# Rotary queries and the scaling of attention weights moved to GpSimd, with a group's rotary queries made first

## The chip, the cores and the metric

The kernel runs on one core of a Trainium2 chip. The metric is the device time of one execution in microseconds; lower is better. The core has five engines that run at the same time, each through its own queue in strict order: TensorE (PE in the profile; its weight loads are PEld), VectorE (DVE), ScalarE (ACT), GpSimd (POOL) and SyncE (SP), which issues the DMAs. An instruction that has to wait for another engine holds up everything behind it on its own queue.

## What is computed

The reference is a trunk of two layers on 256 tokens of width 2048, in fp32: a Conformer convolution module and an MLP, then multi-head latent attention and an MLP, with RMS norms in between. The change lies in the attention layer:

```python
def mla(h, cos, sin, w_in, q_norm_g, kv_norm_g, w_q_up, w_kv_up, w_o):
    down = h @ w_in
    c_q, c_kv, k_pe = jnp.split(down, [Q_LORA_RANK, Q_LORA_RANK + KV_LORA_RANK], axis=-1)
    q = (rms_norm(c_q, q_norm_g) @ w_q_up).reshape(B, S, N_HEADS, QK_NOPE_DIM + QK_ROPE_DIM)
    q_nope, q_pe = jnp.split(q, [QK_NOPE_DIM], axis=-1)
    q_pe = apply_rope(q_pe, cos[:, :, None, :], sin[:, :, None, :])
    k_pe = apply_rope(k_pe, cos, sin)
    kv = (rms_norm(c_kv, kv_norm_g) @ w_kv_up).reshape(B, S, N_HEADS, QK_NOPE_DIM + V_HEAD_DIM)
    k_nope, v = jnp.split(kv, [QK_NOPE_DIM], axis=-1)
...
    s = (jnp.einsum('bqhd,bkhd->bhqk', qn, k_nope)
         + jnp.einsum('bqhr,bkr->bhqk', qp, k_pe)).astype(jnp.float32) * scale
...
    p = jax.nn.softmax(s, axis=-1).astype(v.dtype)
    return jnp.einsum('bqhk,bkhd->bqhd', p, v)
```

There are 16 heads; a head's query has 128 plain columns (`q_nope`) and 64 rotary ones (`q_pe`). The rotary turn of a query's halves x1 and x2 is x1·cos − x2·sin and x2·cos + x1·sin: four multiplications, a subtraction and an addition.

## The kernel before, in words

**Numbers in two parts.** Matrix products are made in fp32r from a high and a low part of each operand, in three products (`mm3`, L178: high·high, low·high, high·low). The high part is a copy on ScalarE (`hi_part`, L186; for weights L154), the low part a subtraction on DVE (`lo_part`, L191; for weights L155). Each weight block is therefore loaded by DMA, then split in two halves (`split_half`, L148), each a ScalarE instruction followed by a DVE instruction. In the convolution, some of the low parts are made on GpSimd (also L155); in the attention layer GpSimd has nothing to do.

**Units and pieces.** The attention weights are listed as `units` in the order in which they are used (L848 to L878). `start_unit` notes that the halves of the unit two places further on are due; `prefetch` (L909) issues those splits, and the load of a unit three further on behind a second half. The 16 heads are treated in four groups of four. For each group there are 14 pieces of TensorE work, each 12 matrix products of 256 columns into one PSUM tile (`acc`, six banks in rotation):

- `qn_piece` (L1000), four: the plain query of one head, and its two parts (L186, L191);
- `qp_piece` (L1015), two: the rotary queries of the group's four heads for one half of the tokens. `rope` (L828) turns them by six DVE instructions of 128 columns (L834 to L839), the four multiplications reading the products from PSUM. `hi_part` and `lo_part` make the two parts, in the tile `qhl`;
- `kv_piece` (L973), eight: keys (L987 to L990, two parts) or values (L995 to L998).

`qp_turn` (L1029) transposes the rotary queries of two heads on TensorE (L1034), and ScalarE copies them into `qpA` and `qpB` (L1043, L1044).

**Heads.** `scores` (L1060) makes a head's 3 × 128 columns of scores, DVE takes the maxima (`mx`, L1075 and L1076) and ScalarE the exponentials with their sums (`pr`, L1078). `weights` (L1083) inverts the sums and scales the exponentials (two DVE instructions, of 128 and 256 columns, L1088). `weights_turn` (L1090) transposes them (L1094) and copies them to `pT` (L1096); `values` (L1098) multiplies them with the values (L1103, L1104) and makes the two parts `oh` and `ol`.

**The order** is written out by hand (`manual_schedule`, L1124 to L1242), and every engine's queue follows it. The pieces of group g + 1 are spread over the heads of group g. One head h issues: scores(h), one piece, the turn of weights(h − 1), for the last two heads of a group `qp_turn`, values(h − 2), the scaling of weights(h), and the rest of its pieces, each followed by a `prefetch` of one half. Before the first head stand group 0's pieces and the first three pieces of group 1. In `q_work` (L1049) the four `qn` pieces come first and the two `qp` pieces second. The pieces of the last group's heads (12 to 15) are those of the output projection.

Of the kernel before, what the change touches and what calls it, by code (L numbers as in the profile page):

```python
# [10 lines left out]
F32 = mybir.dt.float32  # L11
# [7 lines left out]
P = 128  # L19
# [53 lines left out]
def trunk_kernel(  # L73
# [750 lines left out]
    with ExitStack() as cx:  # L824
        at = cx.enter_context(tc.tile_pool(name="at", bufs=1, reuse_waits="tile"))
        at2 = cx.enter_context(tc.tile_pool(name="at2", bufs=2, reuse_waits="tile"))

        def rope(dst, src, t, nh):  # L828

            a, b = src[:, :, 0:HR], src[:, :, HR:DR]  # L830
            cb = cos[:, t : t + 1, :].broadcast_to([P, nh, HR])
            sb = sin[:, t : t + 1, :].broadcast_to([P, nh, HR])
            m = [at2.tile([P, 4, HR], F32, tag=f"m{i}", name=nm("m"), bufs=1)[:, :nh, :] for i in range(4)]
            nc.vector.tensor_tensor(m[0], a, cb, op=ALU.mult)  # L834
            nc.vector.tensor_tensor(m[1], b, sb, op=ALU.mult)
            nc.vector.tensor_tensor(m[2], b, cb, op=ALU.mult)
            nc.vector.tensor_tensor(m[3], a, sb, op=ALU.mult)
            nc.vector.tensor_tensor(dst[:, :, 0:HR], m[0], m[1], op=ALU.subtract)
            nc.vector.tensor_tensor(dst[:, :, HR:DR], m[2], m[3], op=ALU.add)  # L839

        HG = 4
        NG = H // HG
# [7 lines left out]
        def unit(key, srcs, shape):  # L850
            pieces[key] = len(units)
            units.append((srcs, shape))
# [9 lines left out]

        def q_units(g):
            hs = slice(g * HG, (g + 1) * HG)
            unit(("qn", g), [wq4[:, j : j + 1, hs, :DN] for j in range(NJ)], [P, NJ, HG * DN])
            unit(("qp", g), [wq4[:, j : j + 1, hs, DN:] for j in range(NJ)], [P, NJ, HG * DR])

        for g in range(NG):
            if g == 0:
# [145 lines left out]
        def qp_piece(g, t):  # L1015
            key = ("qp", g)
            start_unit(key, t)
            o = acc_tile()[:, : HG * DR]
            ts = slice(t * P, (t + 1) * P)
            for j in range(NJ):  # L1020
                wh, wl = w_at(key, j)
                mm3(o, qh[:, j, ts], ql[:, j, ts], wh, wl, j == 0, j == NJ - 1)
            qp = at2.tile([P, HG, DR], F32, tag="qp", name=nm("qp"))
            rope(qp, o.rearrange("p (h n) -> p h n", h=HG), t, HG)
            hl = qps[g, t] = at2.tile([P, HG, 2, DR], F32R, tag="qhl", name=nm("qhl"))
            hi_part(qp, hl[:, :, 0, :])
            lo_part(qp, hl[:, :, 0, :], hl[:, :, 1, :])

        def qp_turn(g, m):  # L1029

# [16 lines left out]
            return [lambda i=i, c=c: kv_piece(g, i, c) for i in range(HG // 2) for c in range(4)]  # L1047

        def q_work(g):  # L1049
            return [lambda i=i: qn_piece(g, i) for i in range(HG)] + [lambda t=t: qp_piece(g, t) for t in range(T)]  # L1050

        def group_work(g):
            kv = kv_work(g)
# [29 lines left out]
        def weights(h):  # L1083
            pr, zs = prs[h], zss.pop(h)
            nc.vector.reciprocal(zs, zs)
            for t, at_, n in sides:
                q = pr[:, at_ : at_ + n]
                nc.vector.tensor_scalar(q, q, scalar1=zs[:, t : t + 1], scalar2=None, op0=ALU.mult)  # L1088

        def weights_turn(h):  # L1090
            pr = prs.pop(h)
# [32 lines left out]
        with tc.manual_schedule():  # L1124
            for n in range(3):
                u_load(n)
            for n in range(LOOK):
                u_split(n, 0)
                u_split(n, 1)
                u_load(n + 3)  # L1130

            ckv = at.tile([P, T, KR + DR], F32, tag="cx", name="ckv")
            ps = [[acc_tile() for _ in range(2)] for _ in range(T)]
            for k in range(KC):
                u, j = divmod(k, 2)
                start_unit(("kv", u), j)
                prefetch()
                if k == KC - 4:
                    r = rms_rstd(ssq, NNB, D, "n")
                wh, wl = w_at(("kv", u), j)  # L1140
                for t in range(T):
                    for i in range(2):
                        ns = slice(i * NKV, (i + 1) * NKV)
                        mm3(ps[t][i][:, :NKV], xh_kt(k, t), xl_kt(k, t), wh[:, ns], wl[:, ns], k == 0, k == KC - 1)
            for t in range(T):
                for i in range(2):
                    nc.scalar.activation(
                        ckv[:, t, i * NKV : (i + 1) * NKV], ps[t][i][:, :NKV], AF.Copy, scale=r[:, t : t + 1]
                    )
            ps = [acc_tile() for _ in range(T)]  # L1150
            for k in range(KC):
                u, j = divmod(k, 4)
                if j in (0, 2):
                    start_unit(("q", u), j // 2)
                    prefetch()
                wh, wl = w_at(("q", u), j)
                for t in range(T):
                    mm3(ps[t], xh_kt(k, t), xl_kt(k, t), wh, wl, k == 0, k == KC - 1)
                if k == 0:
                    sq = squares(ckv, KR)  # L1160
                if k == 3:
                    normed(ckv, KR, sq)
                    kps = []
                    for t in range(T):
                        kp = at2.tile([P, 1, DR], F32, tag="kp", name=nm("kp"))
                        rope(kp, ckv[:, t : t + 1, KR:], t, 1)
                        hhl = at2.tile([P, 3, DR], F32R, tag="hhl", name=nm("hhl"))
                        for i in range(2):
                            hi_part(kp[:, 0, :], hhl[:, i, :])
                        lo_part(kp[:, 0, :], hhl[:, 0, :], hhl[:, 2, :])  # L1170
                        kps.append(hhl.rearrange("p a b -> p (a b)").bitcast(F32))
                if k == 9:
                    to_T(ckv, 0, kvh_k, kvl_k, g_kv)
                if k == 11:
                    to_T(ckv, 2, kvh_k, kvl_k, g_kv)
                if k == 13:
                    pt = tr_tile()
                    for t in range(T):
                        nc.tensor.transpose(pt[:, t * P : (t + 1) * P], kps[t][:, : 2 * DR], ident)
                        nc.tensor.transpose(pt[:DR, S + t * P : S + (t + 1) * P], kps[t][:, 2 * DR :], ident)  # L1180
                    nc.scalar.activation(kpA, pt[:, :S], AF.Copy)
                    nc.scalar.activation(kpB[:DR, :], pt[:DR, S:], AF.Copy)
            cq = at.tile([P, T, QR], F32, tag="cx", name="cq")
            for t in range(T):
                nc.scalar.activation(cq[:, t, :], ps[t], AF.Copy, scale=r[:, t : t + 1])
            sq = squares(cq, QR)
            gp.append(right_pool("gp", 2))
            work = kv_work(0)
            for w in work[:2]:
                w()  # L1190
                prefetch()
            normed(cq, QR, sq)
            for w in work[2:6]:
                w()
                prefetch()
            to_T(cq, 0, qh_k, ql_k, g_q)
            to_T(cq, 2, qh_k, ql_k, g_q)
            for w in work[6:] + q_work(0):
                w()
                prefetch()  # L1200
            work = group_work(1)
            warm(AF.Exp)
            work[0]()
            for m in range(2):
                qp_turn(0, m)
            for w in work[1:3]:
                prefetch(1)
                w()
            work = work[3:]
            for g in range(NG):  # L1210
                for i in range(HG):
                    h = g * HG + i

                    n = -(-len(work) // (HG - i))
                    todo, work = work[:n], work[n:]
                    scores(h)
                    todo.pop(0)()


                    if h > 0:  # L1220
                        weights_turn(h - 1)
                    if i > 1 and g + 1 < NG:
                        qp_turn(g + 1, i - 2)
                    if h > 1:
                        values(h - 2)
                    weights(h)
                    prefetch(1)
                    for w in todo:
                        w()
                        prefetch(1)  # L1230
                if g + 2 < NG:
                    work = group_work(g + 2)
                elif g + 2 == NG:
                    work = [lambda k=k: o_piece(k) for k in range(H - HG)]
            weights_turn(H - 1)
            values(H - 2)
            for k in (H - 4, H - 3):
                o_piece(k)
            values(H - 1)
            for k in (H - 2, H - 1):  # L1240
                o_piece(k)
            prefetch()  # L1242
# [53 lines left out]
```

## Time and profile before

| | us |
|---|---|
| time, median of 3 runs (lowest, highest) | 2030.07 (2029.39, 2031.12) |
| the profiled execution, its own time | 2029.38 |
| its span, first to last instruction | 2027.6 |
| granted TensorE clock over the span | 0.998 |
| PE busy | 1995.5 |
| DVE busy | 1225.6 |
| ACT busy | 962.6 |
| POOL busy | 173.9 |

The attention layer's groups lie between about 1093 and 1262 us of the span. In a row of the timeline the first number is the start, the second the duration, then engine, line, operation, output<-inputs, partitions and shapes, the count, and in brackets the idle time before it with what ended it. A row of the stretches gives its length, then for each engine busy time and instructions, the granted clock, the DMA's busy share and its rate. A row of the waits gives who waited for whom, the sum, the number of waits and the longest.

### The profile page before, as it was taken

Reading aid. Unit: us, or ns where it says so; the run is one execution under the profiler, and the core shown is the slowest. Engines: PE = TensorE matmul, PEld = TensorE weight load, DVE = VectorE, ACT = ScalarE, POOL = GpSimd, SP = SyncE. Lnnn points to the kernel's source line nnn. Section 1 sums busy time; section 2 is a strip of 40 time slices with the busy share of each in tenths; the row PEclk is TensorE's granted clock in tenths of the full one; section 3 lists DMA queues with packets and bytes.
Section 4 is the critical chain, followed back from the end, with each engine's and each line's share of the span. In section 5 each row is a group of like instructions: output and inputs, shape, how many; then the busy total and the mean of one; then the engine's idle time right before and its main releaser. Section 6 shows DMA issues by size and latency. Waiting matters only on the chain.

```text
span 2027.6 us, 27995 instructions
## 1 busy us (share of the span) xinstructions
PE 1995.5 (98%) x11150; PEld 1747.5 (86%) x11150; DVE 1225.6 (60%) x1858; ACT 962.6 (47%) x1364; POOL 173.9 (9%) x101
## 2 busy tenths in 40 slices
PE   7999999999999999999999899999999999999998
PEld 7999888888888888888889898888888888888886
DVE  5999866665544466555546675665554445565454
ACT  5444665544433354444445554554443334454442
POOL 5887400000000000000000000000000000000000
PEclk9999999999999999999999999999999999999999
DMA  7555355665555666655555335566655566555553
GB/s 235 167 167 166 122 190 171 203 188 187 191 199 191 188 189 192 194 192 187 187 162 175 111 125 180 179 204 189 193 197 188 191 200 191 187 187 190 200 191 104
DMA packets 243267, 367.59 MB, mean 181 GB/s; under 512 B 15416, under 2 KB 89792, under 8 KB 242880
## 3 DMA queue, kind: packets, MB, share of 16 engines
q1 hardware_dynamic: 242400, 364.68, 56.9%
q8 instruction: 87, 1.43, 0.3%
q10 hardware_dynamic: 736, 1.12, 0.2%
q14 instruction: 44, 0.36, 0.1%
HBM read 363.68 MB, written 2.10 MB: 180 GB/s over the span
## 4 chain that ended last, share of the span: by engine, by line
PE 92%; DVE 4%; ACT 2%; issue 1%; DMA 0%; SPq 0%; DVEq 0%; ACTq 0%
PE acc L397 23%; PE acc L180 15%; PE acc L182 15%; PE acc L181 15%; PE acc L398 12%; PE acc L484 3%; PE acc L482 3%; PE acc L483 3%; DVE lo L155 1%; PE sum L515 1%; PE tr L237 1%; ACT hi L154 0%; ACT pr L1078 0%; DMA xs<-in_x 0%; DVE mx L1075 0%
## 5 line engine op out<-in xcount | busy, mean ns | idle before, releaser
L155 DVE TENSOR_TENSOR lo<-raw,hi 128x1024 fp32r<-128x1024 f32 (+1 forms) x628 | 755.3, 1206 | 679.8 <-ACT hi L154 667.3
L154 ACT ACTIVATE hi<-raw 128x1024 fp32r<-128x1024 f32 (+1 forms) x696 | 722.8, 1046 | 788.9 <-PE acc L181 455.3
L397 PE MATMUL acc<-xt,hi 128*128 128x512 f32 x2048 | 710.6, 390 | 0.0
L398 PE MATMUL acc<-xt,lo 128*128 128x256 f32 x2048 | 577.7, 282 | 0.0
L397 PEld LDWEIGHTS acc<-xt,hi 128*128 128x128 f32 x2048 | 384.5, 188 | 80.5
L180 PE MATMUL acc<-hi,gh 128*128 128x512 f32 x1024 | 398.6, 389 | 0.0
L182 PE MATMUL acc<-lo,gh 128*128 128x512 f32 x1024 | 398.4, 389 | 0.0
L181 PE MATMUL acc<-hi,gl 128*128 128x512 f32 x1024 | 398.4, 389 | 0.0
L398 PEld LDWEIGHTS acc<-xt,lo 128*128 128x128 f32 x2048 | 387.1, 189 | 0.1
L182 PEld LDWEIGHTS acc<-lo,gh 128*128 128x128 f32 x1024 | 192.2, 188 | 40.0
L180 PEld LDWEIGHTS acc<-hi,gh 128*128 128x128 f32 x1024 | 192.2, 188 | 39.7
L181 PEld LDWEIGHTS acc<-hi,gl 128*128 128x128 f32 x1024 | 192.2, 188 | 39.7
L549 DVE SCALAR_TENSOR_TENSOR sum<-ub,w_dw,sum 128x256 f32<-128x256 f32 x402 | 167.6, 483 | 4.9 <-ACT sum L518 2.9
L155 POOL TENSOR_TENSOR lo<-raw,hi 128x1024 fp32r<-128x1024 f32 x68 | 161.9, 2403 | 57.8 <-ACT hi L154 57.8
L482 PE MATMUL acc<-xt,hi 128*128 128x256 f32 x512 | 147.3, 288 | 0.0
L484 PE MATMUL acc<-xt,lo 128*128 128x256 f32 x512 | 143.2, 280 | 0.2 <-POOL lo L155 0.2
L483 PE MATMUL acc<-xt,hi 128*128 128x256 f32 x512 | 143.0, 279 | 0.0
L483 PEld LDWEIGHTS acc<-xt,hi 128*128 128x128 f32 x512 | 96.3, 188 | 0.6 <-DVE xt L193 0.2
L482 PEld LDWEIGHTS acc<-xt,hi 128*128 128x128 f32 x512 | 96.3, 188 | 0.4
L484 PEld LDWEIGHTS acc<-xt,lo 128*128 128x128 f32 x512 | 96.2, 188 | 0.4 <-POOL lo L155 0.4
L918 POOL MEMSET pad_kv<- 128x8 f32 x1 | 0.1, 104 | 772.5 <-PE acc L182 772.5
L405 ACT ACTIVATE v<-acc 128x256 f32<-128x256 f32 x128 | 46.4, 382 | 25.3 <-PE acc L398 25.3
(215 smaller groups left out, 1767.8 us busy)
## 6 DMA issues: line engine op xcount, KB each, us to landing
raw<-in_mlp_w SPq DMA_DIRECT2D x256, 1024.0 KB, 5.2
raw<-in_conv_w_pw SPq DMA_DIRECT2D x64, 512.0 KB, 5.0
raw<-in_conv_w_pw SPq DMA_DIRECT2D x16, 1024.0 KB, 5.0
raw<-in_mla_w_o SPq DMA_DIRECT2D x16, 1024.0 KB, 5.6
raw<-in_mla_w_kv_up SPq DMA_DIRECT2D x8, 1024.0 KB, 5.4
raw<-in_mla_w_in SPq DMA_DIRECT2D x8, 576.0 KB, 3.7
raw<-in_mla_w_in SPq DMA_DIRECT2D x4, 1024.0 KB, 5.6
raw<-in_mla_w_q_up SPq DMA_DIRECT2D x16, 256.0 KB, 3.2
```

The costliest lines, as they stand in the source:

```text
L154: nc.scalar.activation(hi, raw[:, js, :], AF.Copy)
L155: eng.tensor_tensor(lo, raw[:, js, :], hi.bitcast(F32), op=ALU.subtract)
L180: nc.tensor.matmul(ps, sh, mh, start=start, stop=False)
L181: nc.tensor.matmul(ps, sl, mh, start=False, stop=False)
L182: nc.tensor.matmul(ps, sh, ml, start=False, stop=stop)
L397: nc.tensor.matmul(ps[b], wh[:, bs], xhl(k), start=k == 0, stop=False)
L398: nc.tensor.matmul(ps[b][:, :S], wl[:, bs], xh(k), start=False, stop=k == KC - 1)
L405: nc.scalar.activation(v[:, b, :], o[:, S:], AF.Copy)
L482: nc.tensor.matmul(o, wh[:, bs], xh(k), start=k == 0, stop=False)
L483: nc.tensor.matmul(o, wh[:, bs], xl(k), start=False, stop=False)
L484: nc.tensor.matmul(o, wl[:, bs], xh(k), start=False, stop=k == KC - 1)
L549: nc.vector.scalar_tensor_tensor(out=out, in0=ubs[c][:, w : w + S], scalar=tap(c, w), in1=pcs[c], op0=ALU.mult, op1=ALU.add)
```

## The change

Three things are changed.

1. The rotary turn of the queries goes to GpSimd. GpSimd's instructions are given SBUF operands only, so a new ScalarE copy first brings the products from PSUM into a tile `qr` of one buffer. The low part of the rotary queries goes to GpSimd as well; the high part stays on ScalarE. `qp` has one buffer instead of two. The keys' rotary turn stays on DVE.
2. The two scaling instructions of each head's weights go to GpSimd; the reciprocal stays on DVE.
3. In a group, the two `qp` pieces come ahead of the four `qn` pieces, and the two units of weights change places in the list. Before the first head, group 0's `qp_turn` comes ahead of group 1's first piece.

```diff
-        def rope(dst, src, t, nh):
+        def rope(dst, src, t, nh, eng):
...
-            nc.vector.tensor_tensor(m[0], a, cb, op=ALU.mult)
-            nc.vector.tensor_tensor(m[1], b, sb, op=ALU.mult)
-            nc.vector.tensor_tensor(m[2], b, cb, op=ALU.mult)
-            nc.vector.tensor_tensor(m[3], a, sb, op=ALU.mult)
-            nc.vector.tensor_tensor(dst[:, :, 0:HR], m[0], m[1], op=ALU.subtract)
-            nc.vector.tensor_tensor(dst[:, :, HR:DR], m[2], m[3], op=ALU.add)
+            eng.tensor_tensor(m[0], a, cb, op=ALU.mult)
+            eng.tensor_tensor(m[1], b, sb, op=ALU.mult)
+            eng.tensor_tensor(m[2], b, cb, op=ALU.mult)
+            eng.tensor_tensor(m[3], a, sb, op=ALU.mult)
+            eng.tensor_tensor(dst[:, :, 0:HR], m[0], m[1], op=ALU.subtract)
+            eng.tensor_tensor(dst[:, :, HR:DR], m[2], m[3], op=ALU.add)
...
         def q_units(g):
             hs = slice(g * HG, (g + 1) * HG)
+            unit(("qp", g), [wq4[:, j : j + 1, hs, DN:] for j in range(NJ)], [P, NJ, HG * DR])
             unit(("qn", g), [wq4[:, j : j + 1, hs, :DN] for j in range(NJ)], [P, NJ, HG * DN])
-            unit(("qp", g), [wq4[:, j : j + 1, hs, DN:] for j in range(NJ)], [P, NJ, HG * DR])
...
-            qp = at2.tile([P, HG, DR], F32, tag="qp", name=nm("qp"))
-            rope(qp, o.rearrange("p (h n) -> p h n", h=HG), t, HG)
+
+            qr = at2.tile([P, HG, DR], F32, tag="qr", name=nm("qr"), bufs=1)
+            nc.scalar.activation(qr, o.rearrange("p (h n) -> p h n", h=HG), AF.Copy)
+            qp = at2.tile([P, HG, DR], F32, tag="qp", name=nm("qp"), bufs=1)
+            rope(qp, qr, t, HG, nc.gpsimd)
             hl = qps[g, t] = at2.tile([P, HG, 2, DR], F32R, tag="qhl", name=nm("qhl"))
             hi_part(qp, hl[:, :, 0, :])
-            lo_part(qp, hl[:, :, 0, :], hl[:, :, 1, :])
+            nc.gpsimd.tensor_tensor(hl[:, :, 1, :], qp, hl[:, :, 0, :].bitcast(F32), op=ALU.subtract)
...
         def q_work(g):
-            return [lambda i=i: qn_piece(g, i) for i in range(HG)] + [lambda t=t: qp_piece(g, t) for t in range(T)]
+            return [lambda t=t: qp_piece(g, t) for t in range(T)] + [lambda i=i: qn_piece(g, i) for i in range(HG)]
...
             for t, at_, n in sides:
                 q = pr[:, at_ : at_ + n]
-                nc.vector.tensor_scalar(q, q, scalar1=zs[:, t : t + 1], scalar2=None, op0=ALU.mult)
+                nc.gpsimd.tensor_scalar(q, q, scalar1=zs[:, t : t + 1], scalar2=None, op0=ALU.mult)
...
             work = group_work(1)
             warm(AF.Exp)
-            work[0]()
             for m in range(2):
                 qp_turn(0, m)
+            work[0]()
```

## What was predicted, before the run

> **What bounds the kernel now.** I read the page's engine line, then busy time by stretch, then PE's waits inside the attention layer.
>
> ```profile
> span 2027.6 us, 27995 instructions
> PE 1995.5 (98%) x11150; PEld 1747.5 (86%) x11150; DVE 1225.6 (60%) x1858; ACT 962.6 (47%) x1364; POOL 173.9 (9%) x101
> ...
> 1118.20:1139.50 21.30, 17.38 (x148) 17.18 (x148) 12.98 (x36) 11.97 (x27) 0.00 (x0) 1.00 0.35 90
> 1139.50:1145.70 6.20, 6.10 (x36) 5.79 (x37) 4.36 (x10) 3.54 (x10) 0.00 (x0) 0.72 0.59 182
> 1145.70:1262.00 116.30, 113.33 (x782) 104.52 (x782) 76.09 (x185) 64.12 (x148) 0.00 (x0) 1.00 0.45 145
> ...
> PE tr L1094 <- DVE pr L1088: 6.6, 3, 4.0
> PE tr L1034 <- DVE qhl L191: 2.3, 1, 2.3
> ```
>
> TensorE is busy 98% of the span, so the end moves only by what TensorE waits. In the attention layer it waits 2.3 us for group 0's rotary queries, and 6.6 us in three waits for scaled weights. After the longest (4.0 us) its granted clock averages 0.72 for 6.2 us, about 1.7 us more. All a gain can take is thus about 10.6 us. GpSimd is empty here and DVE and ScalarE are about 65% and 55% busy: neither is full, but each runs in strict order, and what is late is the head of a queue.
>
> **What the edits cost as work.** DVE and ScalarE rows of before; first number the start, second the duration:
>
> ```profile
> 1121.73 1.06 ACT L154 ACTIVATE hi<-raw 128x1024 fp32r<-128x1024 f32 x1
> 1122.68 0.38 ACT L186 ACTIVATE qTh<-acc 128x256 fp32r<-128x256 f32 x1
> ...
> 1126.62 0.37 ACT L1078 ACTIVATE pr<-acc,mx 128x128 f32<-128x128 f32 x1 [2.35 <-DVE mx L1076]
> ...
> 1127.42 0.38 ACT L186 ACTIVATE qTh<-acc 128x256 fp32r<-128x256 f32 x1
> 1130.20 0.42 ACT L186 ACTIVATE qhl<-qp 128x256 fp32r<-128x256 f32 x1 [2.40 <-DVE qp L839]
> 1130.53 1.04 ACT L154 ACTIVATE hi<-raw 128x1024 fp32r<-128x1024 f32 x1
> 1122.83 1.23 DVE L155 TENSOR_TENSOR lo<-raw,hi 128x1024 fp32r<-128x1024 f32 x1 [2.44 <-ACT hi L154]
> 1123.97 0.42 DVE L191 TENSOR_TENSOR qTl<-acc,qTh 128x256 fp32r<-128x256 f32 x1
> 1124.30 1.22 DVE L155 TENSOR_TENSOR lo<-raw,hi 128x1024 fp32r<-128x1024 f32 x1
> ...
> 1125.77 0.61 DVE L1075 TENSOR_REDUCE mx<-acc 128x1 f32<-128x128 f32 x2
> ...
> 1128.18 0.16 DVE L1085 RECIPROCAL zs<-zs 128x2 f32<-128x2 f32 x1
> 1128.37 0.55 DVE L1088 TENSOR_SCALAR pr<-pr,zs 128x128 f32<-128x128 f32 x2
> 1128.84 0.28 DVE L834 TENSOR_TENSOR m<-acc,cos 128x128 f32<-128x128 f32 x1
> ...
> 1129.83 0.28 DVE L839 TENSOR_TENSOR qp<-m,m 128x128 f32<-128x128 f32 x1
> ```
>
> Instructions follow each other closer than they last, so I use slots, start to start: ScalarE half split 0.95, eviction 0.28, qhl hi 0.33, the two exponentials 0.80; DVE half split 1.14, L191 0.33, from the maximum's start to the exponential 0.85, scaling pair 0.47. A rotary turn on DVE takes 1.27 (1128.84 to 1130.11). A hand-over is 0.04 (1122.79 to 1122.83).
>
> DVE loses eight times 1.27 and a lo part of about 0.42, and sixteen scaling pairs: 13.5 + 7.5 = 21 us. ScalarE gains eight copies out of PSUM (0.38 as L186, slot 0.28). None of this is itself on the path: neither engine is full. The price of GpSimd comes from the convolution:
>
> ```profile
> 107.77 1.30 POOL L689 TENSOR_TENSOR xs<-xs,b 128x512 f32<-128x512 f32 x1
> 109.00 0.14 POOL L496 MEMSET ub<- 128x30 f32 x1
> ...
> 113.44 7.14 POOL L155 TENSOR_TENSOR lo<-raw,hi 128x1024 fp32r<-128x1024 f32 x3 [0.34 <-ACT hi L154]
> ...
> 0.80 0.20 POOL masks.py:197 MEMSET ident<- 128x128 f32 x1
> ...
> 16.94 2.58 POOL L155 TENSOR_TENSOR lo<-raw,hi 128x1024 fp32r<-128x1024 f32 x1 [0.63 <-ACT hi L154]
> ...
> 16.80 3.01 DVE L627 TENSOR_SCALAR xn<-xs,y 128x512 f32<-128x512 f32 x2
> ...
> 21.30 0.86 DVE L627 TENSOR_SCALAR xn<-xs,y 128x512 f32<-128x512 f32 x2
> ```
>
> A two-input slot is 1.23 for 512 columns and about 2.37 for 1024 (7.14 less 2.40, halved), a straight line with 0.09 + 0.00223 a column: 0.375 for 128, 0.66 for 256. A rotary turn is then 6 × 0.375 = 2.25, with tail and two hand-overs **R = 2.45 us**, against DVE's 1.27. No 128-column two-input row exists: below, six memset-like 0.20 give R 1.4; above, six at the 256-column price give 4.1. I take the line. A scaling pair lies between 0.4 (two memsets) and 1.04 (two-input slots); I take 0.65, and only head 0 has it on the path.
>
> Side by side the engines disturb each other: two L627 took 3.01 us while GpSimd's 16.94 ran, alone 0.86, so one was held for the whole GpSimd instruction. Does DVE's half split (two SBUF inputs) likewise hold a rotary multiply that starts after it? No row shows it. Not held: 0. Held: up to 0.9 us at each second turn of a group, because a 1.14 us half split starts just before the copy ends. I take held, as L627 is the nearest row, and keep both ends. The Trainium skill, SBUF — State Buffer, "Who interferes with whom", speaks against this change too: a DVE instruction with two SBUF inputs and a GpSimd instruction that reads SBUF exclude each other, and the later blocks. By it the sum is the held one; without it, the other.
>
> **What moves.** ScalarE's hi part of the rotary queries (L186) stands right behind the new copy, so ScalarE sits still for R twice in every group, and behind it queue the half splits, the evictions that free PSUM banks, and the next exponentials. The same wait for DVE's turn stands in before's list:
>
> ```profile
> ACT qhl L186 <- DVE qp L839: 14.7, 8, 2.5
> ```
>
> That is 1.8 each, with no copy ahead of it; by R it becomes eight times 2.45, about 20. The waits also come earlier: the rotary pieces are first in the group, so for group 1 both stand ahead of head 0's exponentials, where before they stood behind. The weight loads on SP are as many, two units changing places; no wait of this layer names a DMA, and loads run three units ahead: nothing.
>
> PE rows, and three of ScalarE's:
>
> ```profile
> 1105.77 0.28 PE L1010 MATMUL acc<-qh,hi 128*128 128x256 f32 x1
> ...
> 1118.16 1.28 ACT L214 ACT_TABLE_LOAD   x1
> ...
> 1119.83 0.59 ACT L1043 ACTIVATE qpA<-tr 128x512 fp32r<-128x512 f32 x1
> ...
> 1118.13 0.98 PE L1034 MATMUL tr<-ident,qhl 128*128 128x128 f32 x7 [2.25 <-DVE qhl L191]
> ...
> 1121.75 0.22 PE L180 MATMUL acc<-kTh,qTh 128*128 128x128 f32 x1
> ...
> 1122.90 0.28 PE L1010 MATMUL acc<-qh,hi 128*128 128x256 f32 x1
> ...
> 1124.31 0.28 PE L180 MATMUL acc<-hi,qh 128*128 128x256 f32 x1
> ...
> 1139.60 0.70 PE L1094 MATMUL tr<-ident,pr 128*128 128x128 f32 x3 [4.02 <-DVE pr L1088]
> ...
> 1151.06 0.23 PE L180 MATMUL acc<-kTh,qTh 128*128 128x128 f32 x1
> ...
> 1155.00 0.37 ACT L1078 ACTIVATE pr<-acc,mx 128x128 f32<-128x128 f32 x1 [2.28 <-DVE mx L1076]
> ...
> 1177.60 0.61 PE L1094 MATMUL tr<-ident,pr 128*128 128x128 f32 x3 [1.28 <-DVE pr L1088]
> ```
>
> A piece of work is 1.40 us of PE (1122.90 to 1124.31), scores 1.15 (1121.75 to 1122.90), a transpose 0.11 (seven in 0.98, the last one's 0.27 taken off): 0.35 and 0.44 for three and four; values, four matmuls at a twelfth of a piece or less, about 0.4.
>
> Group 0 starts at 1105.77. Its two rotary pieces now end at 1107.2 and 1108.6. From 1107.37: copy 0.38, R, hi 0.33, half split of 512 columns (about 0.5, half of 0.95), copy 0.38, a hold of 0.4 by that short split, R, hi 0.42, lo 0.66 and hand-overs: the turn can start at 1115.5, while PE has its four other pieces done at 1114.2. The wait is 1.3 instead of 2.25, and scores(0) starts at 1120.65 instead of 1121.75: **-1.1**.
>
> Groups 0 to 1. ScalarE reaches the table load about when it did, at 1118.16; 1.4 later follow the four qpA/qpB copies (1.90 from 1119.83 to 1121.73 before), without the eviction at 1119.56: done at 1121.45. Copy to 1121.83, R: hi at 1124.28, half split to 1125.67, copy to 1125.94; the turn is held until 1126.85: hi at 1129.25, half split to 1130.64, DVE's half to 1131.82, L191, maximum at 1132.16, exponential at 1133.0 (before: 1126.62). PE has scores(1) done at 1127.15; the next kv piece lacks that half split and the bank of qn(1,0), waits until 1132.2 (5.0 us) and ends at 1133.6; weights(0) scaled at 1135.45, 1.85 more. Behind exponential(0) stand two evictions and two half splits of each engine: maximum(1) at 1138.15, exponential(1) at 1139.0, eviction, the turned weights, reciprocal at 1140.7, the pair on GpSimd by 1141.4. So weights(1) turn at 1141.45 instead of 1139.5. The wait of 4.0 and its low clock are replaced: the low clock now falls mostly into time when PE waits anyway (I leave 0.6 of 1.7 visible, an estimate). From there to scores(4) PE has two weight turns, two query turns, two values, four pieces and a scores, 9.2: 1151.2 against 1151.06, **+0.15** in all; the 1.1 is spent.
>
> Groups 1 to 2, from scores(4) as 0. Exponential at 3.85 as now (1155.00 less 1151.06); 0.80, copy, R: hi 7.48 to 7.81; evictions of turned weights and values, 384 and 256 columns, 0.65 by L186's 0.28; half split 8.46 to 9.52; copy to 9.79; held until 10.7: hi 13.1; half split to 14.49; eviction, half split; DVE frees the first qn bank at 16.0. PE stands at the kv piece that reuses it at 13.05 (two scores 2.3, six pieces 8.4, two weight turns and values 1.55, and 0.8 for weights(3)): 3.0 us of wait. Eviction, half split and maximum follow on DVE: exponential(5) at 19.5, which frees the bank of scores(6) at 20.35; PE, done with two kv pieces at 18.95, waits another 1.4. From there scores, piece, weight turn, query turn, values, two pieces, scores, piece are 9.1: weights(6) turn at 29.45. Before it was 26.54 (1177.60 less 1151.06), 1.28 of wait included: **+2.9**.
>
> Groups 2 to 3 repeat it (before's 1.28 stands there too): **+2.9**. The later heads have no rotary work and microseconds of slack: 0. After the layer everything shifts whole. Sum 0.15 + 2.9 + 2.9 = **+6.0 us**.
>
> The profiled execution took 2029.38 (span 2027.6 and 1.8 around it); the median is 2030.07, 0.7 above. 2029.4 + 6.0 + 0.7 = **2036.1 us**.
>
> **Rivals.** *Not held*: each second turn is 0.9 shorter, group 1 reaches scores(4) 1.2 earlier, groups 2 and 3 cost 2.1 each: about +3, 2033, within 0.2%. For it: L155 isn't L627.
>
> *Dearer turn*: R near 3.6 (a 0.57 slot, the 32-column pieces of the operands costing extra, or every multiply held). Twice 1.15 in three groups, +7 on the sum: 2043. A low clock after each new 3 us wait (it came after 4.0, not after 2.25) would add up to 2 a group. The Trainium skill, TensorE: Matmul & The Clock Gate, Part 1, puts that point at about 3.4 us of idling, just above my 3.0; the 2.25 and the 4.0 agree with it, and no row lies between.
>
> *Faster*: GpSimd's short instructions cost like DVE's, R about 1.4, nothing held. Then group 0's 2.25 disappears, both 1.28 too, and of the 4.0 and its 1.7 two waits of about 1.8 are left (the chain to the kv piece and to weights(0), two turns shorter): 2.25 + 2.56 + 2.1 = 6.9 less, 2023. It decides from R about 1.85, a slot of 0.28. Against it: both longer GpSimd rows lie on a line that gives 0.375. *The change doesn't act*, i.e. DVE's 21 us and the waits cancel: 2030; nothing singles it out.
>
> **How the numbers follow.** A measurement can tell about 0.2% (4 us) from no change. Chances: forecast, with its spread, 0.47; dearer 0.22; not held 0.16; no effect 0.06; faster 0.09. Of the forecast's 0.47, 0.05 falls below 2034.1, and not held and no effect are within 0.2%. So faster 0.09, same 0.27, slower 0.64. The range runs from near no change to dearer with some low clock: 2029 to 2046.
>
> **What would show it.** Right: GpSimd TENSOR_TENSOR of 128 columns near 0.4 us; ScalarE's qhl hi parts waiting on GpSimd's qp, about 2.4 us each; PE waiting at a kv piece in head 1 (about 5 us) and again in heads 5 and 9, not at L1094 for DVE; a GpSimd multiply beside L155 lasting 1 us or more. Wrong: multiplies of 0.25 us, or ScalarE's eight waits no longer than the 14.7 us of before.

## The result, and the profile after

The changed kernel takes **2042.45 us** (median of 4 runs, 2041.34 to 2043.62) against 2030.12 for the kernel before on the same chip: a ratio of 1.0063 (95% interval 1.0051 to 1.0076), **12.3 us slower**. The forecast was 2036.1, slower, with 2029 to 2046 as its range: the sign and the range hold, but the loss is twice the forecast's 6.0. The profiled execution took 2041.34.

The page's engine line. DVE is 19 us less busy, as the cost of the edits in work had it (21), and PE's idle time has grown:

```profile
span 2039.5 us, 28020 instructions
PE 1999.1 (98%) x11150; PEld 1750.2 (86%) x11150; DVE 1206.5 (59%) x1770; ACT 964.6 (47%) x1372; POOL 239.4 (12%) x189
```

PE's waits in the attention layer: three at the first key piece (L987) of heads 1, 5 and 9, seven for scaled weights, now from GpSimd, and the one of group 0's turn. Their sum is 17.2 us, against 8.9 in the two rows of before that stand in the prediction.

```profile
PE acc L987 <- DVE qTl L191: 10.8, 3, 4.9
PE tr L1097 <- POOL pr L1091: 5.0, 7, 1.6
PE tr L1037 <- POOL qhl L1030: 1.4, 1, 1.4
```

The stretches of heads 5 and 9: besides the waits, the granted clock (the column behind POOL) is low here too, not only behind the wait in head 1 (0.86 from 1126 to 1150). 0.91 over 20 us is 1.8 us of work not done.

```profile
1160.00:1180.00 20.00, 16.70 (x125) 16.16 (x124) 10.73 (x23) 11.52 (x30) 8.20 (x12) 0.91 0.41 120
...
1200.00:1220.00 20.00, 16.31 (x120) 15.56 (x119) 12.35 (x25) 12.07 (x28) 5.71 (x10) 0.91 0.48 158
```

PE's L987 names DVE, but what DVE's queue waited for stands in the list of all engines: 40.2 us for ScalarE's half splits, against 17.5 in the same stretch of before; and ScalarE 25.7 us for GpSimd's turn (14.7 for DVE's before). Before's row first, then after's two:

```profile
DVE lo L155 <- ACT hi L154: 17.5, 16, 2.4
```

```profile
ACT qhl L186 <- POOL qp L839: 25.7, 8, 4.3
...
DVE lo L155 <- ACT hi L154: 40.2, 25, 6.1
```

ScalarE's rows in head 0 show the chain itself. Each copy for GpSimd is made (the second, at 1125.97, is left out here), and ScalarE then sits 2.66 and 3.39 us in front of the high part; the half split (L154) that the key piece of head 1 needs stands behind it:

```profile
1121.66 0.37 ACT L1025 ACTIVATE qr<-acc 128x256 f32<-128x256 f32 x1
1124.69 0.42 ACT L186 ACTIVATE qhl<-qp 128x256 fp32r<-128x256 f32 x1 [2.66 <-POOL qp L839]
...
1129.72 0.42 ACT L186 ACTIVATE qhl<-qp 128x256 fp32r<-128x256 f32 x1 [3.39 <-POOL qp L839]
1130.05 1.04 ACT L154 ACTIVATE hi<-raw 128x1024 fp32r<-128x1024 f32 x1
```

On GpSimd, the groups by form: an instruction of a turn mostly takes 0.46 us; the two instructions of a scaling 0.60 and 1.80 on average (128 and 256 columns), the second of them often lengthened by DVE's work, as a later section shows.

```profile
L1091 POOL TENSOR_SCALAR pr<-pr,zs 128x256 f32<-128x256 f32 x16 | 28.8, 1799 | 0.0
...
L1091 POOL TENSOR_SCALAR pr<-pr,zs 128x128 f32<-128x128 f32 x16 | 9.7, 603 | 78.8 <-DVE zs L1088 57.8 <-PE acc L1076 15.3 <-PE acc L182 5.7
...
L838 POOL TENSOR_TENSOR qp<-m,m 128x128 f32<-128x128 f32 x8 | 3.7, 457 | 0.0
```

### The profile page after: what moved, and what is told of

Its sections match the earlier page's. It is cut to its first block, busy times and chain, and to the rows that moved or that the text cites. A ratio compares the mean times of both kernels' runs of the same rounds, so it can differ in the third digit from the quotient of the medians.

```text
span 2039.5 us, 28020 instructions
## 1 busy us (share of the span) xinstructions
PE 1999.1 (98%) x11150; PEld 1750.2 (86%) x11150; DVE 1206.5 (59%) x1770; ACT 964.6 (47%) x1372; POOL 239.4 (12%) x189
## 4 chain that ended last, share of the span: by engine, by line
PE 93%; DVE 2%; ACT 2%; POOL 1%; issue 1%; DMA 0%; SPq 0%; DVEq 0%; ACTq 0%; POOLq 0%
PE acc L397 23%; PE acc L182 15%; PE acc L181 15%; PE acc L180 15%; PE acc L398 12%; PE acc L484 3%; PE acc L482 3%; PE acc L483 3%; PE sum L515 1%; PE tr L237 1%; ACT hi L154 1%; DVE lo L155 1%; POOL pr L1091 0%; DMA xs<-in_x 0%; PE acc L987 0%
## 5 line engine op out<-in xcount | busy, mean ns | idle before, releaser
L155 DVE TENSOR_TENSOR lo<-raw,hi 128x1024 fp32r<-128x1024 f32 (+1 forms) x628 | 756.8, 1208 | 706.9 <-ACT hi L154 694.9
L154 ACT ACTIVATE hi<-raw 128x1024 fp32r<-128x1024 f32 (+2 forms) x696 | 722.6, 1045 | 789.1 <-PE acc L181 455.3
```

The source lines that it names most:

```text
L154: nc.scalar.activation(hi, raw[:, js, :], AF.Copy)
L155: eng.tensor_tensor(lo, raw[:, js, :], hi.bitcast(F32), op=ALU.subtract)
```

## The experiments

Three theories are told apart. **A**: ScalarE's high part of the rotary queries waits for GpSimd's long turn at the head of ScalarE's queue, and what stands behind it is late; the scaling adds a little. **B**: GpSimd's work itself costs, above all the scaling, which stands between the exponentials and the turn of the weights, and the contention with DVE. **C**: the new order of a group does it. All differences are against the kernel before on the same chip (2029.41 in the first four, 2029.36 in the next four, 2029.67 in the last two).

**Only the scaling on GpSimd** (part 2 of the change):

```diff
-                nc.vector.tensor_scalar(q, q, scalar1=zs[:, t : t + 1], scalar2=None, op0=ALU.mult)
+                nc.gpsimd.tensor_scalar(q, q, scalar1=zs[:, t : t + 1], scalar2=None, op0=ALU.mult)
```

> Only the scaling of the weights goes to GpSimd; rotary turn and order as before. Theory A (ScalarE stands behind GpSimd's rotary turn, and that is most of the 12 us): a small loss, about +3 us, since the three waits for scaled weights of before grow by 1 to 1.5 us each (the pair takes at least 1.5 us in the changed kernel's trace, 0.55 on DVE). Rival B (the scaling on GpSimd, 1.5 to 3.3 us a pair, is the main cost): +8 us or more. Rival C (the new order is the main cost): about 0.

Measured 2034.70, a ratio of 1.0026 (1.0016 to 1.0036): +5.3. PE's waits:

```profile
PE tr L1094 <- POOL pr L1088: 9.4, 8, 2.3
PE tr L1034 <- DVE qhl L191: 2.3, 1, 2.3
```

Three waits for weights (6.6 us) have become eight. The result lies between A's +3 and B's +8: the scaling is dearer than A had it, but it doesn't carry the whole loss, as B would have it.

**Only the rotary turn on GpSimd** (part 1; order and scaling as before): the scaling, `q_units`, `q_work` and the group-0 turn are put back. Against the changed kernel:

```diff
-            return [lambda t=t: qp_piece(g, t) for t in range(T)] + [lambda i=i: qn_piece(g, i) for i in range(HG)]
+            return [lambda i=i: qn_piece(g, i) for i in range(HG)] + [lambda t=t: qp_piece(g, t) for t in range(T)]
...
-                nc.gpsimd.tensor_scalar(q, q, scalar1=zs[:, t : t + 1], scalar2=None, op0=ALU.mult)
+                nc.vector.tensor_scalar(q, q, scalar1=zs[:, t : t + 1], scalar2=None, op0=ALU.mult)
...
+            work[0]()
             for m in range(2):
                 qp_turn(0, m)
-            work[0]()
```

> Only the rotary turn of the queries (with its copy and its low part) goes to GpSimd; scaling on DVE, plain queries first as before. Theory A: +5 us: group 0's turn, now right behind its GpSimd work, waits about 2 us longer than 2.25, and the three waits for weights grow by about 1 us each. Rival B: +1 us or less. Rival C (GpSimd's turn does harm only in the new order): within 1 us of before.

Measured 2042.48, 1.0066 (1.0053 to 1.0079): +13.1, far more than any theory said. PE's waits:

```profile
PE tr L1037 <- POOL qhl L1030: 10.6, 4, 3.8
PE tr L1097 <- DVE pr L1091: 7.0, 3, 4.0
```

In the old order the rotary queries are made last and needed soon, so PE waits for the turned queries themselves: twice at group 0's turn and once each for those of groups 2 and 3, 10.6 us in all. The granted clock is 0.83 from 1120 to 1160, where before has 1.00 and 0.91 in the two halves. The waits for weights, which A had growing, stay as they were (7.0 against 6.6). So this is another wait than the one that A names: it shows that the turn on GpSimd is dear without the scaling, against B's +1, but it doesn't decide between A and C for the changed kernel. The next run does that.

**Only the order** (part 3, all arithmetic on DVE):

```diff
+            unit(("qp", g), [wq4[:, j : j + 1, hs, DN:] for j in range(NJ)], [P, NJ, HG * DR])
             unit(("qn", g), [wq4[:, j : j + 1, hs, :DN] for j in range(NJ)], [P, NJ, HG * DN])
-            unit(("qp", g), [wq4[:, j : j + 1, hs, DN:] for j in range(NJ)], [P, NJ, HG * DR])
...
-            return [lambda i=i: qn_piece(g, i) for i in range(HG)] + [lambda t=t: qp_piece(g, t) for t in range(T)]
+            return [lambda t=t: qp_piece(g, t) for t in range(T)] + [lambda i=i: qn_piece(g, i) for i in range(HG)]
...
-            work[0]()
             for m in range(2):
                 qp_turn(0, m)
+            work[0]()
```

> Only the order: rotary pieces first in a group and group 0's turn ahead of group 1's first piece; all arithmetic on DVE as before. Theory A: faster, about -4 us: group 0's wait of 2.25 goes, and the DVE turn of 1.27 us lets ScalarE go on 1.2 us earlier than GpSimd's, twice a group. Rival B: about 0. Rival C: slower by 3 us or more, as the exponentials of head 0 come late whoever turns the queries.

Measured 2024.05, 0.9973 (0.9962 to 0.9984): **-5.4**, a gain. PE's waits:

```profile
PE tr L1094 <- DVE pr L1088: 2.4, 2, 1.2
PE acc L180 <- ACT pr L1078: 2.2, 2, 1.2
PE acc L180 <- DVE vv L998: 0.4, 1, 0.4
```

The group-0 wait and the 4.0 with its low clock are gone: 8.9 us of waits and 1.7 of low clock have become 4.6 of waits with the clock full (the last row, 0.4, stands in before too). C falls here: the order by itself is no loss. ScalarE still waits 13.6 us for the turn in all; with DVE's 1.27 us it is early enough.

**Turn and order, scaling on DVE** (parts 1 and 3).

```diff
-                nc.gpsimd.tensor_scalar(q, q, scalar1=zs[:, t : t + 1], scalar2=None, op0=ALU.mult)
+                nc.vector.tensor_scalar(q, q, scalar1=zs[:, t : t + 1], scalar2=None, op0=ALU.mult)
```

> The change with the scaling back on DVE. Theory A: +8 us, the waits of PE at the kv pieces (4.9, 2.8, 3.0 us) and the low clock behind them stay, the waits for weights shrink. Rival B: +3 us or less. Rival C: about +10 us.

Measured 2039.42, 1.005 (1.0038 to 1.0063): +10.0. The largest of PE's waits:

```profile
PE acc L987 <- DVE qTl L191: 12.0, 3, 4.9
```

The three L987 waits belong to the turn. The +10 that C named came true by number only, as the order alone is a gain. Against the order alone, the turn costs 15.4 us (from -5.4 to +10.0). The scaling adds 2.3 to it (to +12.3), which is no more than the uncertainty of each of these differences (about 2.5).

**The whole change, with the two parts of the rotary queries issued later.** If A holds, GpSimd may keep all of its work (the rival, B2, is that GpSimd's work and its contention with DVE cost the same wherever the parts are issued), so long as nothing waits for it at the head of ScalarE's queue. The high and low part are made behind the second and the fourth plain piece; the turn works in the copy's tile, which has two buffers.

```diff
-            qr = at2.tile([P, HG, DR], F32, tag="qr", name=nm("qr"), bufs=1)
-            nc.scalar.activation(qr, o.rearrange("p (h n) -> p h n", h=HG), AF.Copy)
-            qp = at2.tile([P, HG, DR], F32, tag="qp", name=nm("qp"), bufs=1)
-            rope(qp, qr, t, HG, nc.gpsimd)
+            qp = at2.tile([P, HG, DR], F32, tag="qr", name=nm("qr"))
+            nc.scalar.activation(qp, o.rearrange("p (h n) -> p h n", h=HG), AF.Copy)
+            rope(qp, qp, t, HG, nc.gpsimd)
             hl = qps[g, t] = at2.tile([P, HG, 2, DR], F32R, tag="qhl", name=nm("qhl"))
-            hi_part(qp, hl[:, :, 0, :])
-            nc.gpsimd.tensor_tensor(hl[:, :, 1, :], qp, hl[:, :, 0, :].bitcast(F32), op=ALU.subtract)
+            late[g, t] = qp, hl
...
             in_parts(o, qTs[g], i)
+            if i in (1, 3):
+                qp_parts(g, i // 2)
```

> The whole change, but ScalarE's high part of the rotary queries (and GpSimd's low part behind it) is issued two and four plain-query pieces later, when GpSimd's turn is long over; the turn writes over the copy, so that two buffers fit. GpSimd does the same work. Theory A (ScalarE standing still behind GpSimd's turn is the loss): the waits at the kv pieces (4.9, 2.8, 3.0 us) go, ScalarE's waits for GpSimd's turn fall from 25.7 us to under 3; the time is that of the order alone (2024) plus the scaling's 3 to 5: 2027 to 2030. Rival B2 (GpSimd's turn costs by its length or by holding DVE, not by who waits for it): 2038 or more.

Measured 2027.06 (11 runs), 0.999 (0.9981 to 0.9999): -2.3, so 14.6 better than the change as it is. PE's waits, and ScalarE's for the turn (25.7 in after):

```profile
PE tr L1103 <- POOL pr L1097: 4.1, 5, 1.5
PE tr L1043 <- POOL qhl L1036: 2.6, 2, 2.3
...
ACT qhl L186 <- POOL qr L839: 1.5, 2, 1.1
```

GpSimd's rows of head 0 in the same run:

```profile
1119.59 0.47 POOL L834 TENSOR_TENSOR m<-qr,cos 128x128 f32<-128x128 f32 x1 [3.02 <-ACT qr L1028]
...
1120.85 1.44 POOL L837 TENSOR_TENSOR m<-qr,sin 128x128 f32<-128x128 f32 x1
1122.37 1.33 POOL L838 TENSOR_TENSOR qr<-m,m 128x128 f32<-128x128 f32 x1
1123.66 0.46 POOL L839 TENSOR_TENSOR qr<-m,m 128x128 f32<-128x128 f32 x1
```

This turn is held twice and lasts 4.53 us (1119.59 to 1124.12), longer than any the forecast worked with, and yet ScalarE doesn't stand still for it. What it still delays is the scaling of weights(0) in GpSimd's own queue: the inverses are ready at 1126.32, the scaling starts at 1127.41, and PE waits 0.99 for it (the pair lasts 3.37, with a half split of DVE beside it). So in this order the loss comes mostly from where ScalarE stands when it waits for the turn, not from how long the turn takes. That is A. The second buffer of the copy is no rival: in the changed kernel ScalarE issues the second copy only behind the first high part, when the first turn is over, and made it at 1125.97 without a wait.

**The same with the scaling on DVE**; beside the diff above:

```diff
-                nc.gpsimd.tensor_scalar(q, q, scalar1=zs[:, t : t + 1], scalar2=None, op0=ALU.mult)
+                nc.vector.tensor_scalar(q, q, scalar1=zs[:, t : t + 1], scalar2=None, op0=ALU.mult)
```

> The same with the scaling back on DVE. Theory A: 2022 to 2025, as the order alone or a little better, since DVE is rid of the turns and nobody waits for GpSimd. Rival B2: 2035 or more.

Measured 2022.21, 0.9963 (0.9951 to 0.9976): -7.2, so the scaling on GpSimd costs 4.9 here. One place is left, group 0's turn:

```profile
PE tr L1043 <- POOL qhl L1036: 2.5, 2, 2.3
```

**The order and the later parts, all arithmetic on DVE.** Does the later issue pay without GpSimd as well? Beside the diff of the order:

```diff
-            hi_part(qp, hl[:, :, 0, :])
-            lo_part(qp, hl[:, :, 0, :], hl[:, :, 1, :])
+            late[g, t] = qp, hl
+
+        def qp_parts(g, t):
+            qp, hl = late.pop((g, t))
+            hi_part(qp, hl[:, :, 0, :])
+            lo_part(qp, hl[:, :, 0, :], hl[:, :, 1, :])
...
+            if i in (1, 3):
+                qp_parts(g, i // 2)
```

> The order alone, all arithmetic on DVE, with the high and low parts issued later as well, so that ScalarE doesn't wait for DVE's turn either (13.6 us in the order alone). Theory A: a little under the order alone, 2021 to 2024; PE's waits of 1.0 to 1.2 us at heads 6 and 10 go. Rival (those waits hang on DVE's queue, not ScalarE's): 2024 as the order alone.

Measured 2019.28 (2018.76 to 2019.58), 0.9949 (0.9935 to 0.9962): **-10.1**, the best of all versions, below the 2021 to 2024 that was expected, and 4.7 better than the order alone. Of the 10.6 us that the prediction set as the most there was to gain, nearly all is gained. PE's waits, 1.6 in all, with the clock full (the 0.4 stands in before too):

```profile
PE tr L1041 <- DVE qhl L191: 1.2, 1, 1.2
PE acc L180 <- DVE vv L999: 0.4, 1, 0.4
```

**The whole change with spare transposes.** Is the low clock behind the new waits a cost of its own? Twenty transposes of the identity that nothing reads fill PE's wait ahead of the first key piece of groups 1 to 3.

```diff
                 vvs[g] = gp[0].tile([P, T, HG * DV], F32, tag="vv", name=nm("vv"))
+                if g > 0:
+                    spare = tr_tile()
+                    for n in range(20):
+                        nc.tensor.transpose(spare[:, n % 4 * P : (n % 4 + 1) * P], ident, ident)
```

> The whole change, with 20 transposes of the identity (about 2.2 us, never read) ahead of the first kv piece of groups 1 to 3, where PE waits 4.9, 2.8 and 3.0 us. They do nothing but keep PE busy. Theory A with the clock as a part of its own: the waits shrink to about 2.7, 0.6 and 0.8, the granted clock stays full behind heads 5 and 9, and the time falls by 3 to 4 us to about 2039. Rival (the low clock falls into time when PE waits anyway): 2042, no change.

Measured 2042.33, 1.0063 (1.005 to 1.0075): +13.0, what the change gives without them. The stretch of head 9 (that of head 5 is alike), and two of PE's waits:

```profile
1200.00:1220.00 20.00, 17.20 (x139) 16.20 (x138) 11.48 (x21) 10.79 (x27) 6.78 (x11) 1.00 0.40 129
```

```profile
PE acc L991 <- DVE qTl L191: 4.2, 3, 2.8
PE acc L180 <- ACT pr L1085: 2.3, 2, 1.1
```

The clock is full there (0.91 in after), and two waits of 1.1 us for the exponentials' bank appear that after doesn't show. From scores(4) to scores(8), and from there to scores(12), this run takes 35.02 and 37.06 us, the changed kernel 35.30 and 37.05. In after, PE worked slowly through the time that it would otherwise have waited. ScalarE's and DVE's chain sets the time of these two stretches, and the low clock is nearly free in them. Behind the wait in head 1 the spare transposes didn't keep the clock (0.88 from 1120 to 1140), so a low clock there isn't shown to be free.

**The two parts of the order, each alone**, all arithmetic on DVE. First only group 0's turn ahead of group 1's first piece:

```diff
-            work[0]()
             for m in range(2):
                 qp_turn(0, m)
+            work[0]()
```

> Only group 0's turn of the rotary queries is put ahead of group 1's first piece; the pieces keep the old order, all arithmetic on DVE. Pieces theory: the gain of 5.4 us of the new order comes from making the rotary queries first. Here they are still the last of group 0, so the turn can't start earlier than at 1118.13 as before, PE waits 2.25 plus the 1.40 of the piece that now stands behind it, and scores(0) starts 1.4 later, with some low clock perhaps: +1.4 to +3. Turn theory: the early turn is what pays, -2 to -5.

Measured 2030.20, 1.0002 (0.9993 to 1.0011): +0.5, no difference that can be told. Then only the order of the units and the pieces, without the early turn:

```diff
+            unit(("qp", g), [wq4[:, j : j + 1, hs, DN:] for j in range(NJ)], [P, NJ, HG * DR])
             unit(("qn", g), [wq4[:, j : j + 1, hs, :DN] for j in range(NJ)], [P, NJ, HG * DN])
-            unit(("qp", g), [wq4[:, j : j + 1, hs, DN:] for j in range(NJ)], [P, NJ, HG * DR])
...
-            return [lambda i=i: qn_piece(g, i) for i in range(HG)] + [lambda t=t: qp_piece(g, t) for t in range(T)]
+            return [lambda t=t: qp_piece(g, t) for t in range(T)] + [lambda i=i: qn_piece(g, i) for i in range(HG)]
```

> Only the order of the pieces and of the two units is changed (rotary pieces first in each group); group 0's turn stays behind group 1's first piece, all arithmetic on DVE. Pieces theory: no wait is left at group 0's turn with or without the early turn, and the waits for scaled weights of 4.0 and 1.28 shrink as with the whole order: -4.5 to -6. Turn theory: 0 to -2.5.

Measured 2025.42, 0.998 (0.9971 to 0.9989): -4.3. The two largest of PE's waits of the first, then of the second:

```profile
PE tr L1094 <- DVE pr L1088: 5.6, 5, 1.7
PE tr L1034 <- DVE qhl L191: 3.4, 2, 2.6
```

```profile
PE tr L1094 <- DVE pr L1088: 2.4, 2, 1.2
PE acc L180 <- ACT pr L1078: 2.3, 2, 1.2
```

The pieces pay: making the rotary queries first takes away group 0's wait and most of those for weights. The gain of the pieces is just under the -4.5 to -6 expected, and can't be told from that of the whole order. The early turn alone makes group 0 wait 3.4 instead of 2.3, as expected, but most of that is given back behind it: the longest wait for weights is 1.7, not 4.0, since the exponential that it hangs on, that of head 1, comes only 0.6 later than before (1138.14 against 1137.51). So the "+1.4 to +3" was wrong: a wait ahead of a later wait on another chain is not simply added to it.

## Why the prediction was right, and where its size came from

**The queue: right.** ScalarE behind GpSimd's turn was the named mechanism, and the later parts show it: the same work on GpSimd without that wait is 14.6 us faster. PE waited 1.4 at group 0's turn against 1.3 (the list above), and 4.94, 2.82 and 2.99 at the three key pieces against 5.0, 3.0 and 3.0:

```profile
1132.73 0.58 PE L987 MATMUL acc<-kvh,hi 128*128 128x256 f32 x1 [4.94 <-DVE qTl L191]
...
1169.50 0.39 PE L987 MATMUL acc<-kvh,hi 128*128 128x256 f32 x1 [2.82 <-DVE qTl L191]
...
1205.05 0.58 PE L987 MATMUL acc<-kvh,hi 128*128 128x256 f32 x1 [2.99 <-DVE qTl L191]
```

**Held: right in group 1, another cause in groups 2 and 3.** GpSimd's first multiplication of group 1's second turn and the half split on DVE beside it:

```profile
1126.41 1.24 POOL L834 TENSOR_TENSOR m<-qr,cos 128x128 f32<-128x128 f32 x1 [0.47 <-ACT qr L1025]
```

```profile
1126.10 1.22 DVE L155 TENSOR_TENSOR lo<-raw,hi 128x1024 fp32r<-128x1024 f32 x1 [6.14 <-ACT hi L154]
```

The multiplication starts 0.31 after the split and lasts 0.78 longer than the 0.46 of the others. The Trainium skill, SBUF — State Buffer, "Who interferes with whom", says that the later of two such instructions blocks; this row agrees. The rival *not held* (2033) falls, though held turns alone, as the later parts showed, needn't cost much. In groups 2 and 3 the first multiplication of the second turn isn't held (it lasts 0.45). There the turn stands behind a scaling pair in GpSimd's own queue, which the prediction doesn't have; in group 2 the copy is done at 1162.18, and the turn starts only at 1163.92, behind this row:

```profile
1161.59 2.37 POOL L1091 TENSOR_SCALAR pr<-pr,zs 128x128 f32<-128x128 f32 x2 [0.51 <-DVE zs L1088]
```

ScalarE waits 4.32 for that turn, where the sum had about 3.3, but had come to it 0.6 earlier than in the sum (0.35 in group 3). That 2.82 and 2.99 agree so well with 3.0 is partly luck.

**Where the 6 missing microseconds are.** The start of scores(4), scores(8) and scores(12), before's rows first (that of scores(4) stands in the prediction):

```profile
1181.98 0.22 PE L180 MATMUL acc<-kTh,qTh 128*128 128x128 f32 x1
...
1212.77 0.22 PE L180 MATMUL acc<-kTh,qTh 128*128 128x128 f32 x1
```

```profile
1120.74 0.22 PE L180 MATMUL acc<-kTh,qTh 128*128 128x128 f32 x1
...
1152.99 0.23 PE L180 MATMUL acc<-kTh,qTh 128*128 128x128 f32 x1
...
1188.29 0.22 PE L180 MATMUL acc<-kTh,qTh 128*128 128x128 f32 x1
...
1225.34 0.22 PE L180 MATMUL acc<-kTh,qTh 128*128 128x128 f32 x1
```

scores(0) starts at 1120.74 (forecast 1120.65). The shift at scores(4) is +1.9 instead of +0.15; groups 1 to 2 add 4.4 and groups 2 to 3 add 6.3, instead of 2.9 each. At scores(12) that makes 12.6 instead of 5.95; the span has grown by 11.9, so 0.7 comes back later.

*The scaling pair* is the first term that failed: "I take 0.65, and only head 0 has it on the path". GpSimd's rows: 1.50 with no half split on DVE beside it, up to 3.33 beside half splits.

```profile
1154.82 1.50 POOL L1091 TENSOR_SCALAR pr<-pr,zs 128x128 f32<-128x128 f32 x2 [4.73 <-DVE zs L1088]
...
1231.51 3.33 POOL L1091 TENSOR_SCALAR pr<-pr,zs 128x128 f32<-128x128 f32 x2 [4.55 <-DVE zs L1088]
```

The upper end of my bounds was 1.04, from a two-input slot that I took for the worst case. PE's rows of the turns of weights(1) and weights(10), after first, then weights(1) of the run with the scaling on DVE:

```profile
1143.36 0.27 PE L1097 MATMUL tr<-ident,pr 128*128 128x128 f32 x1
...
1221.13 0.44 PE L1097 MATMUL tr<-ident,pr 128*128 128x128 f32 x2 [1.61 <-POOL pr L1091]
```

```profile
1141.70 0.33 PE L1097 MATMUL tr<-ident,pr 128*128 128x128 f32 x1
```

weights(1) turn at 1143.36, not at the forecast's 1141.45; with the scaling on DVE they turn at 1141.70. That is nearly all of the 1.8 missing at scores(4). In groups 1 to 2 PE waits 1.0 for weights (0.55 and 0.48) where I had 0.8, in groups 2 to 3 2.5 (0.63, 0.22, 1.61), 1.61 of it at weights(10), which I had at 0.

*A sum that left out work* is the second. For groups 1 to 2 my waits were 0.8 + 3.0 + 1.4 = 5.2, and 1.28 goes: that is +3.9, not +2.9. Before takes 26.54 from scores(4) to weights(6), 25.26 without its wait; my list of pieces made 29.45 - 5.2 = 24.25. So 1.0 us of PE's own work was missing, in both groups. Working with the difference of the waits would have shown it. (Two slips of 0.1 in that sum change nothing: 1155.00 less 1151.06 is 3.94, not 3.85, and 13.05, 3.0 and two pieces make 18.85, not 18.95.)

*The low clock* is the third. The sum has none in groups 2 and 3, and the trace shows one in each (0.91 over 20 us, 1.8 us). The price named for it if it came, "up to 2 a group", is wrong too: it stands in the place of the predicted 1.4 at scores(6), a wait that the spare transposes brought out as 1.1, and costs some 0.4 more than the sum had. 1.0 + 0.2 + 0.4 - 0.2 (the key piece) makes 1.4 of the 1.5 missing in groups 1 to 2, and 1.0 + 1.7 + 0.4 makes 3.1 of the 3.4 in groups 2 to 3; the rest I can't place.

The other rivals: *faster* needed a slot of 0.28, and the slot is 0.42; *the change doesn't act* falls with the measured time; of *dearer turn* only the size (2043) came true, by other terms, which is luck: the turn's slot is 0.42, not 0.57. "The waits also come earlier" was priced as harm. The order alone is a gain of 5.4 us, and the loss of the change is thus 15.4 for the turn and 2.3 for the scaling, less that gain. How much of the scaling's cost is GpSimd's own 1.50 us, how much the holding by DVE and how much the delay of the turns behind it was not measured apart.

## What to carry to other kernels

When work moves to a slower engine, look at the instruction that waits for the result, and at what stands behind it in its queue: here issuing two instructions later was worth 14.6 us with the slow engine, and 4.7 even with the fast one. An edit that bundles a move with a new order can hide a gain in a loss, so run the order alone. And check a sum over a chain against the difference of the waits in it.

## What the runs showed of the hardware

- A GpSimd TENSOR_SCALAR with a scalar per partition costs more than a two-input multiplication of the same size: 0.60 us against 0.46 for 128 columns; the pair, where DVE makes no half split beside it, 1.50 against DVE's 0.55. A 128-column two-input slot is 0.42, start to start (0.375 by the line through 512 and 1024 columns).
- A GpSimd pair can be held for longer than one half split of DVE: 3.33 us beside three half splits in a row, for a pair that takes 1.50 without them, is 1.83 more, and a half split lasts 1.22.
- In the changed kernel a wait of 2.99 us was followed by a granted clock of 0.50 over the next 3 us (1205 to 1208), and in the kernel with only the scaling moved, a wait of 2.26 by 0.57 over 4 us, in the stretch behind it:

```profile
1118.00:1122.00 4.00, 4.00 (x22) 4.00 (x23) 1.09 (x2) 3.99 (x8) 0.00 (x0) 0.57 0.55 143
```

  The Trainium skill, TensorE: Matmul & The Clock Gate, Part 1, puts the point at about 3.4 us of idling; these waits are shorter, so here the measurement decides. In before a wait of 2.25 wasn't followed by a low clock.
